# First stage of a two-layer backbone kernel: folds as rounded products, products streamed by tile, and the context's part moved

## The chip, the cores and the metric

One core of a Trainium2 chip runs the whole program. The metric is the device time of one execution in microseconds (us), and what is compared are medians over several executions. Beside them stands the trace of one profiled execution, whose span, from its first to its last instruction, is somewhat shorter than the device time.

## The reference, cut to what matters

The kernel computes two layers over 1024 latent tokens of 1024 channels, with 256 context tokens as a prefix. The change touches what comes first in the even layer: the modulation of both streams, the products of the input projection that it feeds, and the convolution and recurrence on them. It also touches one thing that belongs to the odd layer, the product of two weight matrices that are folded into one ahead of time (`w_in` with `w_grp`; pooling between them works along tokens only, so that they can be joined).

```python
sc, scc = silu(c), silu(c_ctx)
shift, scale, gate = split(sc @ mod_w[l] + mod_b[l], 3)
hx = rmsnorm(x, norm_g[l]) * (1 + scale) + shift
shift_c, scale_c, _ = split(scc @ mod_w[l] + mod_b[l], 3)
hc = rmsnorm(ctx, norm_g[l]) * (1 + scale_c) + shift_c
# even layer
va, vg, ga, xb, gb = split(hx @ w_in, 5)
y_a = silu(layernorm(conv31(va * sigmoid(vg)))) * silu(ga)
y_b = rglru(xb, h0=rglru_state(hc @ w_in_xb)) * silu(gb)
x = x + gate * (concat([y_a, y_b]) @ w_out)
# odd layer
u = hx1 @ w_in_u
y = (pool(u) - u) @ w_grp * scale * silu(g)
```

`rglru` is a short convolution of four taps, two gates from products with small matrices per head, and a scan in both directions; the latent scan starts from the state at which the context's ends.

## The kernel before

Channels lie on partitions: a tile is 128 channels by 1024 tokens, and KT = 8 of them make a stream. Exact enough products are made of rounded numbers (fp32r): both operands are split into a high part (a cast on ACT) and a low part (a subtraction on DVE or POOL), and three matmuls hi·hi, hi·lo and lo·hi are summed in PSUM. I call such a product a rounded triple. Some products are plain fp32 matmuls instead.

**The first stage** has an order that Tile's scheduler made from the code. It loads x tile by tile and sums its squares; broadcasts the silu of the two conditions c (cL for the latent, cC for the context) over the partitions with eight fp32r matmuls of one row; takes 24 dot products of a row block of `mod_w` with cL or cC on DVE (`modulation`, L353; twelve blocks, two conditions each) and computes the last two of each eight rows of shift and scale on PE (`mod_row`, L372 and L378); makes rstd of x as root products ms_x (L211); scales and shifts x into hi and lo parts h0h, h0l (`modulate`, L388 to L392); does the same for the context (`modulate_ctx`, L401 and L443); computes the decay rates of the recurrence (`decay_rates`, from L172); and folds two of four groups of the odd layer's weights in plain fp32 (`fold_whole`, L285; `grp` is graw, the other factor wu), which PE does whenever nothing else is ready. Then come the latent and context products of xb for j = 0 (L133 to L135).

**The loop over j = 0..7** has an order written by hand: `on(engine, ...)` issues each instruction behind the last one of its engine, and the profile puts all of it down to line L510, the line of that helper. A turn j runs on PE vg_j, va_j, xbc_{j+1} (the context's 256 columns), and then the gates of j between the products of xb_{j+1}. On DVE it does the four-tap convolution into uc, u_j = va · sigmoid(vg), the scans of tile j-1 and, in between, steps of the 31-tap convolution of earlier tiles. These steps are handed out by `fill(n)`: it runs n steps of whichever tile's convolution is under way, and does nothing as long as no tile is whole. The eight dots of the modulation's gate rows, on tiles called l, stand in turn j = 0.

Behind the loop come gb and wob products on PE with fixed `fill` counts in them. Where the layernorm of the convolution needs its mean, every step that is left is run:

```python
while ended[0] < KT:
    fill(1)
```

and `ln_mean` sums the eight tiles with a matmul called mu. From there on PE has nothing to do before that sum.

PSUM has eight banks: four in a rotating pool, a pair called xb (`wide`), and two single banks c0, c1, in which the convolution is summed. SP issues almost all DMA transfers; in the first stage `load` chains them in the order of the code.

Of the kernel before, what the change touches and what calls it, by code (L numbers as in the profile page):

```python
# [55 lines left out]
def body(ctx, tc, xT, ctxT, cc, ccol, modT, modW, win, gw, wout, wu, grp, wg, wo1, small, edge, ident, outT):  # L56
# [37 lines left out]

    def banks(name, n):
# [73 lines left out]
    def decay_rates():  # L169
        nc.scalar.activation(sa, lam, AF.Abs)  # L170
        nc.scalar.activation(sa, sa, AF.Exp, scale=-1.0)
        nc.vector.tensor_scalar(out=sb, in0=sa, scalar1=2.0, scalar2=None, op0=add)  # L172
        nc.vector.reciprocal(sb, sb)
        nc.vector.tensor_tensor(out=sz, in0=sa, in1=sb, op=mult)
        nc.vector.tensor_tensor(out=sb, in0=sz, in1=sz, op=mult)
        nc.vector.memset(sa, 1.0 / 17.0)
        for n in range(7, -1, -1):
            nc.vector.tensor_tensor(out=sa, in0=sa, in1=sb, op=mult)
            nc.vector.tensor_scalar(out=sa, in0=sa, scalar1=1.0 / (2 * n + 1), scalar2=None, op0=add)
        nc.vector.tensor_tensor(out=sa, in0=sa, in1=sz, op=mult)  # L180
        nc.vector.tensor_scalar(out=sb, in0=lam, scalar1=-1.0, scalar2=0.0, op0=mult, op1=ALU.max)
        nc.vector.scalar_tensor_tensor(out=sa, in0=sa, scalar=2.0, in1=sb, op0=mult, op1=add)
        nc.vector.tensor_scalar(out=chalf, in0=sa, scalar1=4.0, scalar2=None, op0=mult)
        nc.vector.tensor_scalar(out=cneg, in0=sa, scalar1=-8.0, scalar2=None, op0=mult)
# [86 lines left out]
    def fold_whole(g, out_tile, g_tile, w_tile):  # L271
        gs = []
        for i in range(2):
            raw = g_tile(f"graw_{g}_{i}")
            load(raw, grp[g, i])
            gs += [raw[:, 0:H], raw[:, H:D]]
        yield
        for kp in range(KT // 2):
            w = w_tile(f"wu_{g}_{kp}")
            load(w, wu[g, kp])  # L280
            for s in range(2):
                ps = psum(f"fold_{g}_{kp}_{s}")
                for i in range(4):
                    kc = slice(i * 2 * P + s * P, i * 2 * P + (s + 1) * P)
                    nc.tensor.matmul(ps, w[:, kc], gs[i], start=(i == 0), stop=(i == 3))  # L285
# [12 lines left out]
    cth = [cpool.tile([P, D], F32R, name=f"cth{i}") for i in range(2)]
    ctl = [cpool.tile([P, D], F32R, name=f"ctl{i}") for i in range(2)]
    cL = cpool.tile([P, D], F32, name="cL")  # L300
    hh, hl, ch, cl = [], [], [], []
    with ExitStack() as sctx:
        fpool = sctx.enter_context(tc.tile_pool(name="fpool", bufs=6))
        gpool = sctx.enter_context(tc.tile_pool(name="gpool", bufs=4))
        spool = sctx.enter_context(tc.tile_pool(name="spool", bufs=1))

        def fo_tile(name):
            return fpool.tile([P, H], F32, tag="fo", name=name)

# [24 lines left out]
        def sumsq(acc_, v, n, first, name, eng):
            if first:
                nc.scalar.activation(acc_[:, :n], v, AF.Square)
            else:
                q = ttile(name)
                nc.scalar.activation(q[:, :n], v, AF.Square)
                eng.tensor_tensor(out=acc_[:, :n], in0=acc_[:, :n], in1=q[:, :n], op=add)  # L340

        junk = spool.tile([P, D], F32, name="junk")

        def modulation(k, between=lambda: None):
            raws_ = []
            for m in (k, KT + k):
                raws_.append(dtile(f"mod0_{m}"))
                load(raws_[-1], modT[0, m])
                if m == k:
                    between()  # L350
            for m, raw in zip((k, KT + k), raws_):
                for i, vec in enumerate((cL, cC)):
                    nc.vector.scalar_tensor_tensor(out=junk, in0=raw, scalar=1.0, in1=vec, op0=mult, op1=mult,  # L353
                                                   accum_out=m0[:, i, m : m + 1])
            nc.vector.scalar_tensor_tensor(out=a0[:, :, k], in0=m0[:, :, KT + k], scalar=mb1[:, k : k + 1],
                                           in1=col(O_NG + k).to_broadcast([P, 2]), op0=add, op1=mult)
            v = m0[:, :, k]
            nc.vector.tensor_tensor(out=v, in0=v, in1=col(O_MB + k).to_broadcast([P, 2]), op=add)

        idx = spool.tile([P, P], F32, name="idx")
        ccv = spool.tile([P, KT, 2], F32, name="ccv")

        def mod_row(j):
            ps = psum(f"modr_{j}")[:2, : KR * P]
            for q in range(KT // KW):
                raw = dtile(f"modw_{j}_{q}")
                load(raw[:, : KW * KR * P], modW[j, q])
                for e in range(KW):  # L370
                    k = KW * q + e
                    nc.tensor.matmul(ps, ccv[:, k], raw[:, e * KR * P : (e + 1) * KR * P],  # L372
                                     start=(k == 0), stop=(k == KT - 1))
# [1599 lines left out]
```

## Time and profile before

| what | us |
|---|---|
| time, median of three executions (lowest to highest) | 1289.47 (1287.24 to 1290.38) |
| span of the profiled execution | 1287.8 |
| first fold matmul | starts at 8.97 |
| vg, va and xbc of j = 0 | 92.30, 105.96, 116.84 (start) |
| vg of j = 1 | 137.56 (start) |

A time is that of the device; the profile's own execution is one more run. Its page gives each engine's busy time, its share of the span and its number of instructions; the span in forty slices with a digit for tenths; and the chain of work that ended last, followed back from the end to whatever released each piece. A group names the source line, the engine, the operation, out<-in, the shape and the count, then total busy us, mean ns of one, and the idle time of that engine just before them with what ended it. In the time line of an engine a row is start, duration, what it is, and in square brackets the wait before it. A plain fp32 matmul of 512 columns leaves two records.

### The profile page before, as it was taken

What the parts mean: (1) busy time and instruction counts of PE and PEld (TensorE: products, weight loads), DVE (VectorE), ACT (ScalarE), POOL (GpSimd) and SP (SyncE); (2) the same over time, 40 slices, a digit from 0 to 9 for tenths busy, and PEclk for the clock granted to TensorE, in tenths of its full rate; (3) what the DMA queues carried; (4) which work ended last, traced back from release to release, by engine and by line L of the source; (5) the groups of instructions that cost most, each with busy time, mean ns of one, the idle gap of its engine ahead of it and who ended that gap; (6) DMA issues with size and microseconds to landing.
All of it is one profiled execution on the core that took longest, in us unless ns stands there. A gap on an engine that the chain in (4) does not pass through costs nothing.

```text
span 1287.8 us, 15841 instructions
## 1 busy us (share of the span) xinstructions
PE 1271.1 (99%) x5650; PEld 1027.5 (80%) x5650; DVE 1141.3 (89%) x1775; ACT 640.6 (50%) x941; POOL 354.3 (28%) x180
## 2 busy tenths in 40 slices
PE   8999999999999999999999999999999999999997
PEld 4468888888888888888887888888888888878886
DVE  7979999999999999988789667999999997887876
ACT  5343656666657623227426345834444444654543
POOL 3063655675558603443220023000000000000002
PEclk9999999999999999999999999999999999999999
DMA  9934111121212133543555356243333324777723
GB/s 371 358 114 157 58 41 63 44 74 42 66 41 90 50 115 107 168 147 113 172 174 192 127 185 203 87 155 127 110 132 131 123 96 157 245 247 258 296 83 131
DMA packets 83075, 181.87 MB, mean 141 GB/s; under 512 B 7858, under 2 KB 27826, under 8 KB 82996
## 3 DMA queue, kind: packets, MB, share of 16 engines
q1 hardware_dynamic: 74548, 176.67, 40.1%
q10 hardware_dynamic: 8448, 4.20, 1.1%
q8 instruction: 44, 0.72, 0.2%
q14 instruction: 35, 0.29, 0.1%
HBM read 136.79 MB, written 44.04 MB: 140 GB/s over the span
## 4 chain that ended last, share of the span: by engine, by line
PE 86%; DVE 6%; DMA 5%; ACT 1%; issue 1%; SPq 0%; POOL 0%; POOLq 0%; DVEq 0%; ACTq 0%
PE vg L510 7%; PE wob L510 7%; PE gb L510 7%; PE va L510 7%; PE xb L510 6%; PE g L510 4%; PE fold L285 3%; PE ga L510 2%; PE qb_v L1000 2%; PE qb_v L1001 2%; PE qb_v L998 2%; PE xbc L510 2%; PE qb_g L1000 2%; PE qb_g L1001 2%; PE qb_g L998 2%; DMA x<-xT 1%
## 5 line engine op out<-in xcount | busy, mean ns | idle before, releaser
L510 DVE SCALAR_TENSOR_TENSOR conv<-u,sm,conv 128x505 f32<-128x505 f32 (+6 forms) x224 | 153.9, 748 | 0.9
L1762 POOL TENSOR_TENSOR o<-x,rr 128x256 f32<-128x256 f32 (+1 forms) x10 | 9.4, 971 | 445.7 <-ACT rr L1698 443.8
L510 POOL TENSOR_TENSOR l<-l,l 128x1280 f32<-128x1280 f32 (+1 forms) x23 | 64.0, 2798 | 91.8 <-DVE l L510 65.5
L510 ACT ACTIVATE l<-g,sm 128x512 f32<-128x512 f32 (+1 forms) x96 | 58.7, 619 | 57.7 <-PE g L510 57.0
L285 PE MATMUL fold<-graw,wu 128*128 128x512 f32 x128 | 58.0, 614 | 2.3 <-DMA wu<-wu 2.3
L102 ACT CAST wq_g<-wr_g 128x512 fp32r<-128x512 f32 x48 | 28.3, 622 | 48.4 <-DVE wr_g L979 17.6
L285 PEld LDWEIGHTS fold<-graw,wu 128*128 128x128 f32 x128 | 25.1, 198 | 33.7 <-issue 32.7
L510 PE MATMUL vg<-h0h,wl_vg 128*128 128x512 f32 x128 | 50.0, 390 | 0.0
L510 PE MATMUL wob<-ybh,wh_wob 128*128 128x512 f32 x128 | 49.9, 390 | 0.0
L510 PE MATMUL vg<-h0h,wh_vg 128*128 128x512 f32 x128 | 49.8, 389 | 0.0
L510 PE MATMUL gb<-h0l,wh_gb 128*128 128x512 f32 x128 | 49.8, 389 | 0.0
L510 PE MATMUL gb<-h0h,wh_gb 128*128 128x512 f32 x128 | 49.8, 389 | 0.0
L510 PE MATMUL wob<-ybh,wl_wob 128*128 128x512 f32 x128 | 49.8, 389 | 0.0
L510 PE MATMUL vg<-h0l,wh_vg 128*128 128x512 f32 x128 | 49.8, 389 | 0.0
L510 PE MATMUL wob<-ybl,wh_wob 128*128 128x512 f32 x128 | 49.8, 389 | 0.0
L510 PE MATMUL va<-h0h,wh_va 128*128 128x512 f32 x128 | 49.8, 389 | 0.0
L510 PE MATMUL va<-h0l,wh_va 128*128 128x512 f32 x128 | 49.8, 389 | 0.0
L510 PE MATMUL va<-h0h,wl_va 128*128 128x512 f32 x128 | 49.8, 389 | 0.0
L510 PE MATMUL gb<-h0h,wl_gb 128*128 128x512 f32 x128 | 49.8, 389 | 0.0
L510 DVE TENSOR_TENSOR_SCAN l<-l,l 128x256 f32<-128x256 f32 (+1 forms) x32 | 48.7, 1521 | 1.1
L103 POOL TENSOR_TENSOR wl_wu<-wr_wu,wh_wu 128x1024 fp32r<-128x1024 f32 x8 | 19.2, 2417 | 106.9 <-ACT wh_wu L102 104.4
L510 POOL TENSOR_TENSOR l<-l,uc 128x1280 f32<-128x1280 f32 x16 | 48.1, 3032 | 0.0
(642 smaller groups left out, 4344.0 us busy)
## 6 DMA issues: line engine op xcount, KB each, us to landing
mod<-modT SPq DMA_DIRECT2D x20, 512.0 KB, 5.5
x_part<-xp SPq DMA_DIRECT2D x32, 256.0 KB, 3.1
mod<-modT SPq DMA_DIRECT2D x32, 256.0 KB, 3.1
wr_v<-wfold SPq DMA_DIRECT2D x16, 512.0 KB, 4.0
wr_g<-wg SPq DMA_DIRECT2D x16, 512.0 KB, 4.2
wr_wo<-wo SPq DMA_DIRECT2D x16, 512.0 KB, 4.6
y_b<-y SPq DMA_DIRECT2D x24, 256.0 KB, 3.4
y_t<-y SPq DMA_DIRECT2D x24, 256.0 KB, 2.9
```

What stands on the lines that cost most here:

```text
L102: return (nc.scalar.copy(hi, src), eng.tensor_tensor(out=lo, in0=src, in1=hi.bitcast(F32), op=sub))
L103: eng.tensor_tensor(out=lo, in0=src, in1=hi.bitcast(F32), op=sub))
L285: nc.tensor.matmul(ps, w[:, kc], gs[i], start=(i == 0), stop=(i == 3))
L510: last[eng] = f(*args, **kw)
L998: nc.tensor.matmul(ps, hi, xh[k], start=(first and k == 0), stop=False, skip_group_check=not first)
L1000: nc.tensor.matmul(ps, hi, xl[k], start=False, stop=False, skip_group_check=not first)
L1001: mm = nc.tensor.matmul(ps, lo, xh[k], start=False, stop=(k == KH - 1), skip_group_check=not first)
L1762: nc.gpsimd.tensor_tensor(out=outs[k // per][:, k % per], in0=x1[k][:, cols], in1=rr, op=mult)
```

## The change

1. The two folds become rounded triples: 192 fp32r matmuls where 64 fp32 ones were. `grp` and wu are split: casts on ACT, the four low parts of `grp` on DVE, the eight of wu on POOL.
2. c and c_ctx are broadcast by two DMAs of 512 KB, and their silu stays in PSUM (`cvec`), where the early dots read it; SBUF copies cL and cC serve the late ones. All modulation rows are dots on DVE, 32 of them; `mod_row` is gone.
3. xb0, vg0 and va0 run together as a stream over the eight x tiles, each tile's 18 matmuls as soon as its parts are there. For x tiles 1, 3 and 5 the high and low parts are made by two ACT operations and POOL.
4. The context's modulation, its xb products and its gates stand behind the latent gates of j = 0 and the products of xb1; vg1 is in front of these gates. The decay rates, wsum and the gate rows' dots come behind the stream.
5. The convolution's two banks are one tile `cw`. The loop starts at j = 1.
6. The whole of it goes through `on`, so that it has a written order on each engine. `fill` asks for 1 step in what was turn j = 0 (22 before) and for 20 in turn j = 1 (37 before). In the turns from j = 2 on, and behind the loop, it asks for what it asked before.

```diff
     def banks(name, n):
-        if n % 2:
-            t = wide(name)
-            return [t[:, h] for h in HALF]
-        return [pc.tile([P, H], F32, tag=f"c{i}", name=f"{name}_{i}") for i in range(2)]
+        t = wide(name) if n % 2 else wide2(name)
+        return [t[:, h] for h in HALF]
...
-                    nc.tensor.matmul(ps, w[:, kc], gs[i], start=(i == 0), stop=(i == 3))
...
+    def fold_part(n, s, part, between=()):
+        g = n // 4
+        w = fw[n][part == 2]
+        for i in range(4):
+            kc = slice(i * 2 * P + s * P, i * 2 * P + (s + 1) * P)
+            hi, lo = gpair[g][i // 2]
+            x = lo if part == 1 else hi
+            pe(fps_[n][s], w[:, kc], x[:, HALF[i % 2]], start=(part == 0 and i == 0), stop=(part == 2 and i == 3))
...
+    def split_w(name, out=None):
+        raw = wraw.pop(name)
+        hi, lo = out or [wpool.tile([P, D], F32R, tag=t, name=f"{t}_{name}") for t in ("wh", "wl")]
+        cast(hi, raw)
+        gp(out=lo, in0=raw, in1=hi.bitcast(F32), op=sub)
+        return hi, lo
...
+    def mod_dots(m, vecs=(0, 1)):
+        for i in vecs:
+            vec(nc.vector.scalar_tensor_tensor, out=mraw[m] if i else junk, in0=mraw[m], scalar=1.0,
+                in1=(cL, cC)[i] if late[0] else cvec[i], op0=mult, op1=mult, accum_out=m0[:, i, m : m + 1])
...
+    for k in range(KT):
+        if k < KT - 1:
+            scale_x(k + 1)
+            high_x(k + 1)
+        low_x(k)
...
+        for p, part in order:
+            (hi, lo), ps = prods[p]
+            for h in range(2):
+                pe(ps[h], (lo if part == 1 else hi)[:, kc], (hl if part == 2 else hh)[k][:, HALF[h]],
+                   start=(k == 0 and part == 0), stop=(k == KT - 1 and part == 2))
...
+    for m in (6, KT + 6, 7, KT + 7):
+        mod_dots(m, (1,))
+    mod_ready(1, 0, KT)
...
+    for h in range(2):
+        all_of(mm3_fixed(vg1[h], wnext_vg, (hh, hl), HALF[h]))
...
+    decay_rates()
...
+    at_rest()
+    fill(1)
+    xc = psum("xbc0")[:, :C]
+    all_of(mm3_fixed(xc, w, (ch, cl), slice(0, C)))
...
+    all_of(gate_steps(0, (gwh, gwl), (uh, ul), gates, ((0, C),)))
...
+    for j in range(1, KT):
...
-            fill(3)
+        fill(3 if j > 1 else 0)
...
-            fill(4)
+        fill(4 if j > 1 else 0)
...
-                fill((10, 6)[h])
+            fill((10, 6)[h] if j > 1 else 3)
...
-            fill(19 if state is None else 5 if final else 8)
+        fill(5 if final else 8)
```

The order of the instructions at three places follows. A row is line, operation, out<-in and shape; numbers behind names tell tiles apart, and `x2` stands for two in a row.

PE before, where the folds end and xb of j = 0 begins (all of h0h and h0l, for both halves, goes by before vg0):

```order
L285 MATMUL fold_3_1_644<-graw_0_425,wu_3_634 128x512 x2
L285 MATMUL fold_3_1_644<-graw_1_427,wu_3_634 128x512 x2
L133 MATMUL xb_680<-h0h_461,wh_xb_675 128x512
L134 MATMUL xb_680<-h0l_462,wh_xb_675 128x512
L135 MATMUL xb_680<-h0h_461,wl_xb_676 128x512
L133 MATMUL xb_680<-h0h_487,wh_xb_675 128x512
```

PE now, at the same place (ms_x is the root product of rstd, dg_x its diagonal from DVE; h0h_659 and h0h_679 are the high parts of x tiles 0 and 1):

```order
L274 MATMUL ms_x_589<-dg_x_621,ones 128x512
L274 MATMUL ms_x_590<-dg_x_624,ones 128x512
L274 MATMUL fold_1_588<-g1h_159,wl_571 128x512 x2
L274 MATMUL fold_1_588<-g1h_161,wl_571 128x512 x2
L274 MATMUL xb_685<-h0h_659,wh_xb_633 128x512 x2
L274 MATMUL vg_0_687<-h0h_659,wh_vg_643 128x512
L274 MATMUL vg_1_688<-h0h_659,wh_vg_643 128x512
L274 MATMUL va_686<-h0h_659,wh_va_661 128x512 x2
...
L274 MATMUL va_686<-h0h_659,wl_va_662 128x512 x2
L274 MATMUL xb_685<-h0h_679,wh_xb_633 128x512 x2
```

The root products have moved to the last quarter of the last fold, and behind it each product takes tile after tile instead of product after product.

DVE now, between two tiles of the stream (m_132 holds the modulation's rows, a_133 the scales, mod_5, mod_13 and mod_4 are row blocks):

```order
L274 SCALAR_TENSOR_TENSOR h0l_682<-x_202,m_132,h0h_659 128x1024
L274 SCALAR_TENSOR_TENSOR junk,m_132<-mod_5_580,cL 128x1024
L274 SCALAR_TENSOR_TENSOR x_359<-x_359,a_133,ms_x_589 128x512
L274 SCALAR_TENSOR_TENSOR x_359<-x_359,a_133,ms_x_590 128x512
L274 SCALAR_TENSOR_TENSOR junk,m_132<-mod_13_582,cL 128x1024
L274 SCALAR_TENSOR_TENSOR mod_4_519,m_132<-mod_4_519,cC 128x1024
```

The late dots, on cL and cC, have moved in between the parts that PE's stream takes.

DVE before, in turn j = 1, from u_0 on (u_861; uc_941 is the four-tap convolution of tile 1, the conv rows are the steps that `fill` hands out):

```order
L510 TENSOR_TENSOR u_861<-va_1_888,sg_1_801 128x512
L510 SCALAR_TENSOR_TENSOR edge_junk,edges<-u_861,sm 128x8
L510 TENSOR_TENSOR cL<-u_861 128x512
L510 TENSOR_SCALAR conv_0_943<-u_861,sm 128x512
L510 TENSOR_SCALAR conv_1_944<-u_861,sm 128x512
L510 SCALAR_TENSOR_TENSOR conv_0_943<-u_861,sm,conv_0_943 128x505
L510 SCALAR_TENSOR_TENSOR uc_941<-xbc_916,sm,uc_941 128x254
L510 SCALAR_TENSOR_TENSOR uc_941<-xbc_916,sm,uc_941 128x255 x2
L510 SCALAR_TENSOR_TENSOR conv_1_944<-u_861,sm,conv_1_944 128x504
```

DVE now, from u_0 (u_942) on:

```order
L274 TENSOR_TENSOR u_942<-va_686,sg_1_931 128x512
L274 SCALAR_TENSOR_TENSOR mod_6_647,m_132<-mod_6_647,cC 128x1024
L274 SCALAR_TENSOR_TENSOR mod_14_649,m_132<-mod_14_649,cC 128x1024
...
L274 SCALAR_TENSOR_TENSOR l_934,m_132<-l_934,cL 128x1024
...
L274 TENSOR_SCALAR sb<-sa 128x16
...
L274 TENSOR_TENSOR cL<-u_942 128x512
L274 TENSOR_SCALAR conv_1186<-u_942,sm 128x512
L274 SCALAR_TENSOR_TENSOR uc_928<-xbc_1188,sm,uc_928 128x254
```

Ahead of the first step of a convolution stand the context's dots, those with l and the decay rates; then one step, and the context's taps (uc_928<-xbc). Over the whole program both orders have 416 rows of convolution on DVE. From u_7 up to the layernorm's mean it is 197 rows before and 240 now, and the additions to lnsum there are 6 and 8.

More of the change, by code (lines that the diff above doesn't have):

```diff
@@ new lines, in square_add @@
+    def square_add(k, h):
+        f = dict(out=acc[h], in0=acc[h], in1=xq.pop((k, h)), op=add)
+        if h and k > 1 or k > 5:
+            vec(nc.vector.tensor_tensor, **f)
+        else:
+            gp(**f)
+    chain[0] = nc.sync.dma_start((graw.setdefault((0, 0), dtile("graw_0_0"))), grp[0, 0])
+    act(sb[:, 0:1], eps_l, AF.Silu)
+    busy = psum("busy")
+    for _ in range(20):
+        pe(busy[:, :P], ones, ones, start=True, stop=True)
+    load_g(0, 1)
+    load_fold(0)
+    load(cx[0], cc[0].partition_broadcast(P))
@@ new lines, in body @@
+    load_w("vg0", win[KT])
+    load_w("va0", win[0])
+    fold_out(5, 1)
+    fold_mm(6)
+    square(6)
+    square_add(6, 0)
+    square_add(6, 1)
+    square(7)
+    square_add(7, 0)
+    square_add(7, 1)
+    fw[7] = split_w(7)
+    fold_out(6, 0)
+    for t in range(4):
+        fold_store(t)
+    load_mod(5)
+    load_mod(KT + 5)
+    fold_out(6, 1)
+    mod_dots(4, (0,))
+    fold_banks(7)
+    rx = [psum(f"ms_x{h}") for h in range(2)]
+    n = H // P
+    fold_mm(7, range(5), {1 + h: [lambda h=h, c=c: pe(rx[h][:, c : c + 1], acc[h][:, c * P : (c + 1) * P],
+                                                      ones[:, 0:1], start=True, stop=True) for c in range(n)]
+                          for h in range(2)})
@@ new lines, in body @@
+    for h in range(2):
+        act(roots[:, h * n : (h + 1) * n], rx[h][:, :n], AF.Sqrt, bias=eps_r)
+    diags = []
+    for h in range(2):
+        r, t = roots[:, h * n : (h + 1) * n], ttile(f"dg_x{h}")
+        vec(nc.vector.reciprocal, out=r, in_=r)
+        vec(nc.vector.tensor_tensor, out=t.rearrange("p (c t) -> p c t", t=P),
+            in0=idx.unsqueeze(1).to_broadcast([P, n, P]), in1=r.unsqueeze(2).to_broadcast([P, n, P]), op=mult)
+        diags.append(t)
+    for h in range(2):
+        pe(rx[h], ones, diags[h], start=True, stop=True)
@@ new lines, in body @@
+    for i in range(2):
+        gp(out=ctl[i], in0=cx[i], in1=cth[i].bitcast(F32), op=sub)
+    load_w("va1", win[1], wr_tile("wr_va1"))
+    wva = split_w("va1", [xtile(f"w{i}_va1", F32R) for i in "hl"])
+    for m in range(2 * KT, 2 * KT + 4):
+        lrow_dots(m)
+        lrows[m + 4] = lrow(m + 4)
+    decay_rates()
+    vec(nc.vector.tensor_tensor, out=wsum, in0=taps[:, :, 0 : 2 * NT : 2], in1=taps[:, :, 1 : 2 * NT : 2], op=add)
+    L = [ltile(i, f"l{i}") for i in range(6)]
+    gates, roots = L[:4], L[4:]
@@ new lines, in body @@
+    xb = wide("xb1")
+    steps = (x for h in range(2) for x in mm3_fixed(xb[:, HALF[h]], wnext, (hh, hl), HALF[h]))
+    done = 0
+    for n, _ in enumerate(gate_steps(0, (gwh, gwl), (uh, ul), gates, ((C, H), (C + H, H)))):
+        while done < 16 * (n + 1) // 8:
+            next(steps)
+            done += 1
+    all_of(steps)
+    for m in range(2 * KT + 4, 3 * KT):
+        lrow_dots(m)
+    vec(nc.vector.tensor_tensor, out=m0[:, 0, 2 * KT :], in0=m0[:, 0, 2 * KT :], in1=col(O_MB + 2 * KT, KT), op=add)
@@ new lines, in body @@
+        (r0, i0, r1, i1), (e, f) = state[2], state[3]
+        gates, roots = [e, f, r0, r1], [i1, i0]
+        now = j, uc, gates, roots
+        done = 0
+        for n, _ in enumerate(gate_steps(j, (gwh, gwl), (uh, ul), gates)):
+            while done < 16 * (n + 1) // 12:
+                next(steps)
+                done += 1
+            if n == 9:
+                w = raw_split(raw, name)
+                rec_input(now, 0)
+        all_of(steps)
+        fill(5 if final else 8)
+        state, uc = now, ucn
```

893 lines of the change are left out of this document (485 added, 408 removed).

## The prediction

> **What bounds the kernel now.** I read the page first (busy time, the slices, the chain that ended last), then the chain piece by piece, the groups of instructions of the first 300 us, and at last the time lines of single engines where a term of the sum needs them.
>
> ```profile
> PE 1271.1 (99%) x5650; PEld 1027.5 (80%) x5650; DVE 1141.3 (89%) x1775; ACT 640.6 (50%) x941; POOL 354.3 (28%) x180
> ...
> PE   8999999999999999999999999999999999999997
> ...
> DVE  7979999999999999988789667999999997887876
> ...
> PE 86%; DVE 6%; DMA 5%; ACT 1%; issue 1%; SPq 0%; POOL 0%; POOLq 0%; DVEq 0%; ACTq 0%
> ```
>
> PE is busy 99% of the span, so time is won only by less work on PE and lost by every wait put on it. But DVE's digits are 9 in slices 4 to 16 as well (32.2 us each): from 130 to 547 us a second engine has no room either. That decides this case.
>
> PE's first stage, from the page, the chain, the groups and PE's time line:
>
> ```profile
> L285 PE MATMUL fold<-graw,wu 128*128 128x512 f32 x128 | 58.0, 614 | 2.3 <-DMA wu<-wu 2.3
> ...
> 46.27 27.66 PE fold L285 x64
> ...
> 148.44 10.88 PE va L510 x48
> ...
> 180.04 11.15 PE vg L510 x48
> ...
> L372 PE MATMUL modr<-modw,ccv 128*2 128x256 f32 x32 | 7.2, 379 | 0.0
> L378 PE MATMUL modt<-idx,modrow 2*128 2x2 f32 x8 | 1.2, 251 | 0.5 <-ACT modrow L375 0.5
> L211 PE MATMUL ms_x<-dg_x,ones 128*128 128x512 f32 x4 | 2.0, 618 | 1.5 <-DVE dg_x L208 1.5
> ```
>
> The va at 148.44 is that of j = 1, the vg at 180.04 that of j = 2. From va1 on both programs give PE the same matmuls in the same order, and from j = 2 on the loop is the same code. So the sum has two parts: when vg2 starts, and what is late after it.
>
> **What PE saves.** An fp32 fold matmul leaves two records: 128 at 27.66/64 = 0.432 us are 55.3 us. A rounded one costs 10.88/48 = 0.227 us; 192 are 43.5. Gain 11.8. The modulation rows go: 7.2 + 1.2 = 8.4. The waits for wu (2.3) and for modrow (0.5) go with their instructions. Together 23.0 us. The eight matmuls of the c broadcast ran before the first fold, which waited for its load; its operands are now split first, so I leave the fold's start alone (a us either way). With no new wait va1 would start at 148.4 - 23.0 = 125.4.
>
> **What it puts on DVE and POOL.** Eight more modulation dots (32 for 24), low parts of g on DVE, and of wu, xb0, vg0, va0 and three x tiles on POOL, beside each other. What that does, the trace shows at one place, in DVE's and POOL's time lines:
>
> ```profile
> 104.93 1.22 DVE L510 SCALAR_TENSOR_TENSOR l<-l,cL 128x1024 f32<-128x1024 f32 x1
> 106.07 3.98 DVE L510 SCALAR_TENSOR_TENSOR l<-l,cL 128x1024 f32<-128x1024 f32 x1
> 109.98 3.40 DVE L510 SCALAR_TENSOR_TENSOR l<-l,cL 128x1024 f32<-128x1024 f32 x1
> 113.31 2.30 DVE L510 SCALAR_TENSOR_TENSOR l<-l,cL 128x1024 f32<-128x1024 f32 x1
> ...
> 105.31 3.66 POOL L510 TENSOR_TENSOR ul<-uc,uh 128x1280 fp32r<-128x1280 f32 x1 [3.32 <-ACT uh L510]
> 108.92 3.38 POOL L510 TENSOR_TENSOR wl_xb<-wr_xb,wh_xb 128x1024 fp32r<-128x1024 f32 x1
> 112.26 2.27 POOL L510 TENSOR_TENSOR wl_gw<-wr_gw,wh_gw 128x512 fp32r<-128x512 f32 x1
> ...
> 124.58 14.76 DVE L510 SCALAR_TENSOR_TENSOR conv<-u,sm,conv 128x504 f32<-128x504 f32 x22
> ...
> 134.99 2.41 POOL L510 TENSOR_TENSOR wl_vg<-wr_vg,wh_vg 128x1024 fp32r<-128x1024 f32 x1 [20.45 <-ACT wh_vg L510]
> ```
>
> Alone a dot takes 1.22. Beside POOL the same dot takes 2.3 to 4.0, and each POOL subtraction is about one dot longer than alone (2.37, below): they run in turn. The convolution taps, whose sum is in PSUM, keep 14.76/22 = 0.67, and POOL's 2.41 at 134.99 is as short beside them as anywhere. So I count **in turn** what DVE does from SBUF alone and all of POOL, and leave out DVE operations with an operand in PSUM. By the taps' row the early dots, which read c from PSUM, are free; the late ones, on cL and cC, are not. [...]
>
> Prices of the pieces, from the groups by shape:
>
> ```profile
> L388 DVE SCALAR_TENSOR_TENSOR x<-x,a,ms_x 128x512 f32<-128x512 f32 x16 | 10.8, 744 | 0.5 <-PE ms_x L211 0.5
> L392 DVE SCALAR_TENSOR_TENSOR h0l<-x,m,h0h 128x1024 fp32r<-128x1024 f32 x8 | 10.5, 1335 | 0.0
> L443 DVE TENSOR_TENSOR cx<-cx,ssqc 128x1024 f32<-128x1024 f32 x2 | 2.4, 1222 | 0.0
> L178 DVE TENSOR_TENSOR sa<-sa,sb 128x16 f32<-128x16 f32 x8 | 1.4, 175 | 0.3
> L103 POOL TENSOR_TENSOR wl_xb<-wr_xb,wh_xb 128x1024 fp32r<-128x1024 f32 x1 | 2.4, 2371 | 0.0
> L401 POOL TENSOR_SCALAR cx<-cx,a,m 128x256 f32<-128x256 f32 x8 | 5.2, 670 | 7.6 <-DVE cx L443 7.6
> L340 POOL TENSOR_TENSOR ssq<-ssq,xsq 128x512 f32<-128x512 f32 x7 | 10.3, 1473 | 18.2 <-ACT xsq L339 18.1
> L391 ACT ACTIVATE h0h<-x,m 128x1024 fp32r<-128x1024 f32 x8 | 9.1, 1147 | 6.5 <-DVE x L388 6.3 <-DMA wfold<-fo 0.2
> L510 ACT ACTIVATE l<-l,cneg 128x1280 f32<-128x1280 f32 x8 | 10.5, 1361 | 0.0
> L510 ACT ACT_TABLE_LOAD x13 | 16.7, 1283 | 0.2
> L510 POOL TENSOR_TENSOR l<-l,l 128x1280 f32<-128x1280 f32 x8 | 23.6, 2965 | 11.6 <-ACT l L510 11.6
> ```
>
> **New waits of PE, one by one**, each as its two ends and the value taken.
>
> Folds: PE waits where a weight's low part is later than the 5.4 us (24 x 0.227) of matmuls on the weight before. POOL needs 2.4 for one and has the square sums of x besides, up to 1.5 each, in turn with DVE's splits and sums. It keeps up on average, not at each weight. 0 to 4; I take 2.
>
> Start of the stream: the root products of rstd are now queued ahead of the last quarter of the last fold. Behind them DVE scales two halves (2 x 0.74) and ACT makes the first high part (1.15): 2.6, with the fold's 0.9 as cover, and the second vg bank waits for the cast of the last fold, behind that on ACT (about 1). 2 to 3.5; 2.5.
>
> Stream: 144 matmuls are 32.6 us. In turn beside them stand on POOL seven low parts (16.6) and the four sums of the context's squares (three of 1.5 at most, one of half that: 4.5), on DVE five low parts and ten late dots (15 x 1.22 = 18.3; their 1.34 in the groups holds waiting) and some small ones (1): 40.4. The scaling of x (14 x 0.74 = 10.4) reads ms_x in PSUM and runs beside POOL. Each tile needs its two dots, its scaling and its parts in that order, so PE waits for the sum: 40.4 - 32.6 = 8. Without taking turns DVE's 30 and POOL's 21 both fit under PE's 32.6. 0 to 9; 8.
>
> Context: xbc0 and the context gates of j = 0 found their input ready; the work on it lay under the folds and xb0. Now it stands behind the stream, and in DVE's fixed order so do the dots with l and decay_rates, all ahead of the context's taps. Counted in turn: on DVE four ctx dots and eight with l (12 x 1.22 = 14.6), two scalings (2.4), some 30 of 0.175 (5); on POOL the low parts of xb1 and va1 (4.7), of u and the gate weights (3.0 and 1.2, by width), the eight adds (5.4) and two low parts of the context (4.8): 41 us, of which a little lies after the gates. PE has 33.0 of work there (vg1 10.9, gates and xb1 16.3, xbc 5.7). That is 6 to 8. Dots, adds, casts, xbc, taps, cast of u, low part and gates follow each other through four engines, which adds some microseconds, while the evictions of the latent gates are queued on ACT behind the two context casts, so that PE's banks come free late. With the order of before, 0; by this count up to 16; I take 11.
>
> Gates of j = 1: queued behind them on PE is all of j = 2. They wait for the recurrence of j = 0, which must give its buffers back: two tanh, two exp, two roots (6 x 1.36), two table loads (2.6), two squares on POOL (5.9): 16.7 us from the context gates on. Before, vg1 and va1 (21.8) lay over that; now vg1 has been moved ahead and only va1 and an xbc (13.8) are left. 0 to 4; 3.5.
>
> DMA: the stage loads the same sixteen modulation tiles' worth (twelve and four of modW before), and two broadcasts of c more, 512 KB each. They are hidden as long as about 37 transfers of 0.52 MB arrive before the stream, near 60 us; at the rate of the next row they take 47.5. Were that cover gone, va0 would be late by the difference, a few us. I take 0. SP's stores of the last folds stand ahead of the loads of vg1 and xb1, which have 20 us to spare.
>
> ```profile
> 30.00:40.00 10.00, 8.46 (x40) 4.31 (x39) 9.65 (x23) 2.65 (x5) 0.00 (x0) 1.00 1.03 408
> ```
>
> (A row of the table by stretch: busy us of PE, its loads, DVE, ACT and POOL, the granted clock, the DMA share, GB/s.)
>
> Sum 2 + 2.5 + 8 + 11 + 3.5 = 27.0; 27.0 - 23.0 = **+4**: vg2 at 184.
>
> **What is late after vg2.** The convolution is done on DVE in steps that `fill` hands out; up to the end of j = 1 there were 59, now 21. No later fill is larger. The 38 steps, and two additions to the layernorm sums that were POOL's, come where everything is emptied: ahead of the layernorm mean. DVE's and PE's time lines there:
>
> ```profile
> 414.66 0.69 DVE L510 TENSOR_TENSOR u<-va,sg 128x512 f32<-128x512 f32 x1 [0.81 <-PE va L510]
> ...
> 531.96 18.95 DVE L510 SCALAR_TENSOR_TENSOR conv<-u,sm,conv 128x505 f32<-128x505 f32 x28
> ...
> 565.54 3.13 DVE L510 TENSOR_TENSOR lnsum<-lnsum,u 128x512 f32<-128x512 f32 x2
> ...
> 569.11 0.69 DVE L510 TENSOR_TENSOR mu0l<-lnsum,mu0h 128x512 fp32r<-128x512 f32 x1
> ...
> 573.67 0.39 PE L510 MATMUL mu<-mu0h,ones_r 128*128 128x512 f32 x1
> ```
>
> At 414.66 DVE waits for va7: it is level with PE there, so what it was spared in j = 0 and 1 is no lead that it could still have. A step is 18.95/28 = 0.677; 38 are 25.7, the two additions 1.4: 27.1. DVE had the mean ready at 569.8, PE came for it at 573.7: 3.9 are free. So 23.2; the lnsum pair took 3.13 instead of 1.4 beside POOL, which would then be idle: 21.4. I take 22, from 18.5 (DVE also uses its short waits there) to 23.5. All of PE's wob is issued by then, so it stands.
>
> [...]
>
> **Sum.** The profiled span is 1287.8, 1.7 under the median of 1289.5. 1287.8 + 4 + 22 + 1.7 = **1316** (rounded up from 1315.5).
>
> **Rivals.** A: DVE and POOL hardly hinder each other in the new order. Stream 0, context 2: 2 + 2.5 + 2 + 3.5 - 23 = -13, vg2 at 167; the mean still waits: 1289.5 - 13 + 22 = **1298**. For it: taps and scaling are exempt, the first dots read PSUM. Against: the rows at 106 to 116.
> B, faster: the written order keeps PE fed. The stage's saving stands (23, and 1 from an earlier first fold), the gates of j = 1 are covered, and the mean waits 18.5: 1289.5 - 24 + 18.5 = **1284**. It decides where va1 starts: in this case at 124.4; each us later is one lost, and past 126 nothing measurable is left. For it: PE waited little in the stage of before. Against: 16.7 us of gate chain over 13.8 of PE, which ask for 3 alone.
> C: as B, but with the mean's wait at its full 23.5 us: 1289.5 - 24 + 23.5, about **1290**, no change.
> D: the stage doesn't do what the title says; the order starves PE at every step, all terms at their upper ends: 36.5 - 23 = 13.5 and 23.5 at the mean: **1327**.
>
> **Chances.** Forecast (1306 to 1325) 0.62, A (1292 to 1305) 0.19, C 0.07, B 0.07, D 0.05. The range 1292 to 1325 leaves out B, C and D, a little under 0.2. A measurement tells 0.3% (3.9 us) from no change: faster 0.07, same 0.07, slower 0.86.
>
> **What would show it.** Folds of 192 records at 0.23; va1 near 149 (A: 132, B: 124); dots of 2 to 4 us on cL and cC between 60 and 130; an idle PE ahead of the context gates; one wait of about 22 us ahead of `mu`, released by DVE. Were that wait missing, the step on the deferred convolution would be wrong, whatever the total.

## The result, and the profile after

| | time, us (lowest to highest) | span of the profiled execution |
|---|---|---|
| before | 1288.43 (1287.24 to 1290.38) | 1287.8 |
| changed | 1353.38 (1351.39 to 1359.61) | 1352.2 |

The change makes the kernel slower: the ratio is 1.051, with an interval of 1.0484 to 1.0535. The median of before is here that of four executions, one more than in the table ahead of the prediction. The direction was forecast, the size was not: 1353 lies beyond the 1327 of the worst rival.

The page of the changed kernel, the lines that answer to those shown of before, and the granted clock:

```profile
PE 1270.8 (94%) x5700; PEld 1046.8 (77%) x5700; DVE 1189.1 (88%) x1793; ACT 652.2 (48%) x947; POOL 378.8 (28%) x186
...
PE   8987989989999999972999999999999999999997
...
DVE  5898799999999999999868975998999998787976
...
PEclk9989999999999999995999999999999999999999
...
PE 58%; DVE 19%; issue 9%; ACT 5%; POOL 4%; DMA 4%; SPq 0%; POOLq 0%; ACTq 0%; DVEq 0%
```

PE is busy for as long as before in a span that is 64.4 us longer, and its share of the chain falls from 86% to 58%; DVE's rises from 6% to 19%. The digits 7 and 2 in PE's row are a hole near 600 us. The view of the waits names the holes (PE's line, who released it, us in total, times, longest):

```profile
PE mu L274 <- DVE mu0h L274: 34.8, 1, 34.8
PE vg L274 <- POOL wl_vg L274: 9.7, 5, 3.5
PE g L274 <- ACT l L274: 9.2, 2, 7.9
PE xb L274 <- POOL h0l L274: 4.8, 1, 4.8
PE gb L274 <- POOL wl_gb L274: 3.2, 1, 3.2
```

Two of these stand in no term of the prediction: weights' low parts late for vg, five times, and for gb. Cut at PE's landmarks (starts from PE's time line, us), the 64.4 us lie here:

| stretch | before | after | more | forecast |
|---|---|---|---|---|
| start to vg of j = 2 | 179.9 | 186.1 | 6.2 | 4 |
| turns j = 2 to 7, to the start of gb | 234.9 | 251.2 | 16.3 | 0 |
| gb and wob, to the wait ahead of `mu` | 158.9 | 162.5 | 3.6 | 0 |
| the wait ahead of `mu` | 0.0 | 34.8 | 34.8 | 22 |
| from `mu` to the end | 714.1 | 717.6 | 3.5 | 0 |

The rows at which the turns begin and end, of before and then of after:

```profile
179.88 0.39 PE L510 MATMUL vg<-h0h,wh_vg 128*128 128x512 f32 x1
...
414.74 0.40 PE L510 MATMUL gb<-h0h,wh_gb 128*128 128x512 f32 x1
```

```profile
186.12 0.39 PE L274 MATMUL vg<-h0h,wh_vg 128*128 128x512 f32 x1
...
437.31 0.40 PE L274 MATMUL gb<-h0h,wh_gb 128*128 128x512 f32 x1
```

The row of the turns starts the search. From j = 2 on both programs give PE the same matmuls and ask for the same `fill`. Yet this is how DVE ran the steps of the long convolution there, in time lines of one turn (start, duration, and the count that the row gathers):

```profile
229.25 10.04 DVE L510 SCALAR_TENSOR_TENSOR conv<-u,sm,conv 128x504 f32<-128x504 f32 x15
```

That was before; this is after:

```profile
242.75 11.79 DVE L274 SCALAR_TENSOR_TENSOR conv<-u,sm,conv 128x511 f32<-128x511 f32 x15
```

10.04/15 = 0.669 a step, and now 11.79/15 = 0.786. The groups give one step a mean of 750 ns either way: no step became longer, but they no longer overlap. DVE's written order tells why, here three rows of tile 3 of before and three of after (the number behind a name tells buffers apart; DVE counts on a semaphore what it has done, and in square brackets stand the count that the row waits for and the one to which it raises it):

```
SCALAR_TENSOR_TENSOR conv3_0_2235<-u3_1867,sm_115,conv3_0_2235 128x505 [waits for 345, raises to 347]
SCALAR_TENSOR_TENSOR conv3_1_2236<-u3_1867,sm_115,conv3_1_2236 128x504 [waits for 346, raises to 348]
SCALAR_TENSOR_TENSOR conv3_0_2235<-u3_1867,sm_115,conv3_0_2235 128x506 [waits for 347, raises to 349]

SCALAR_TENSOR_TENSOR conv3_2674<-u3_1966,sm_115,conv3_2674 128x505 [waits for 368, raises to 369]
SCALAR_TENSOR_TENSOR conv3_2674<-u3_1966,sm_115,conv3_2674 128x504 [waits for 369, raises to 370]
SCALAR_TENSOR_TENSOR conv3_2674<-u3_1966,sm_115,conv3_2674 128x506 [waits for 370, raises to 371]
```

The rows go by turns to the left and the right half of the sum. Before, these halves were two tiles, and a step waited for the step two rows back: the row that raises the count to 347 waits for 345. As one tile `cw` each step waits for the row just ahead of it, though the halves share no element. My theory after the result: 0.12 us a step is lost there, which a DVE that is busy 155 of 160 us has no room for; POOL's low parts, queued behind additions that wait for DVE's scans, get late, and PE waits. The rival was that the deferred steps and the first stage alone make the time.

One such wait, in the time line of POOL and then of PE:

```profile
276.22 2.37 POOL L274 TENSOR_TENSOR l<-l,l 128x1024 f32<-128x1024 f32 x1 [16.44 <-DVE l L274]
278.56 2.35 POOL L274 TENSOR_TENSOR wl_vg<-wr_vg,wh_vg 128x1024 fp32r<-128x1024 f32 x1
```

```profile
277.11 0.39 PE L274 MATMUL vg<-h0l,wh_vg 128*128 128x512 f32 x1
280.96 0.50 PE L274 MATMUL vg<-h0h,wl_vg 128*128 128x512 f32 x1 [3.46 <-POOL wl_vg L274]
```

POOL stands idle for 16.44 us with the low part of vg's weight next in its queue, until DVE's scan lets the addition ahead of it go; the low part ends at 280.9 and PE's third matmul goes.

### The profile page after: what moved, and what is told of

The parts are those of the page before. It is cut to its first block, busy times and chain, and to the rows that moved or that the text cites. A ratio compares the mean times of both kernels' runs of the same rounds, so it can differ in the third digit from the quotient of the medians.

```text
span 1352.2 us, 15957 instructions
## 1 busy us (share of the span) xinstructions
PE 1270.8 (94%) x5700; PEld 1046.8 (77%) x5700; DVE 1189.1 (88%) x1793; ACT 652.2 (48%) x947; POOL 378.8 (28%) x186
## 4 chain that ended last, share of the span: by engine, by line
PE 58%; DVE 19%; issue 9%; ACT 5%; POOL 4%; DMA 4%; SPq 0%; POOLq 0%; ACTq 0%; DVEq 0%
DVE conv L274 6%; PE vg L274 5%; POOL l L274 2%; PE wob L274 2%; ACT l L274 2%; PE va L274 2%; PE ga L274 2%; PE ga L131 2%; PE ga L129 2%; PE ga L130 2%; PE qb_g L1204 1%; PE qb_g L1206 1%; PE qb_g L1207 1%; PE qb_v L1204 1%; PE qb_v L1207 1%
## 5 line engine op out<-in xcount | busy, mean ns | idle before, releaser
L274 DVE SCALAR_TENSOR_TENSOR conv<-u,sm,conv 128x505 f32<-128x505 f32 (+6 forms) x224 | 168.0, 750 | 6.4
L274 PE MATMUL xb<-h0l,wh_xb 128*128 128x512 f32 x128 | 50.3, 404 | 5.3 <-POOL h0l L274 4.8
L274 DVE SCALAR_TENSOR_TENSOR conv<-cL,wsum,conv 128x506 f32<-128x506 f32 (+3 forms) x70 | 52.5, 750 | 2.2
L274 PE MATMUL xb<-h0h,wh_xb 128*128 128x512 f32 x128 | 49.9, 400 | 1.9 <-ACT h0h L274 1.9
L274 PE MATMUL xb<-h0h,wl_xb 128*128 128x512 f32 x128 | 49.7, 398 | 0.0
```

What stands on the lines that cost most here:

```text
L274: last[eng] = f(*args, **kw)
```

## The experiments

### The first four: the tile, the deferred steps, and the turn-taking

**e1_two_banks** is the changed kernel with the convolution's sum in two one-bank tiles again. Only the stream's product at the start still uses the wide tile, from a pool that is closed before the first convolution.

```diff
     def banks(name, n):
-        t = wide(name) if n % 2 else wide2(name)
-        return [t[:, h] for h in HALF]
+        if n % 2:
+            t = wide(name)
+            return [t[:, h] for h in HALF]
+        return [pcs[0].tile([P, H], F32, tag=f"c{i}", name=f"{name}_{i}") for i in range(2)]
...
+    pwide.close()
+    pcs[0] = ctx.enter_context(tc.tile_pool(name="pcs", bufs=1, space=PSUM))
```

> The changed kernel with one thing undone: the convolution is summed in two separate single-bank tiles again instead of in the two halves of one tile cw. Theory S (serial steps: with one tile each step of the convolution waits for the step just before it, 0.78 us apart instead of 0.67): steps come 0.67 apart again, vg2 stays near 186, the turns j = 2 to 7 shrink from 44 to 47 us to about 43, PE's wait ahead of mu falls from 34.8 to about 20, and the time from 1353 to 1318 to 1328. Theory F (the late start of the turns and POOL's late weight parts make the loop slow, whatever the steps take): turns stay at 44 to 47, the time stays at 1345 to 1355.

Measured: 1332.09 us (1331.31 to 1332.46), ratio 1.032 (1.0297 to 1.0343). So 21.3 us of the loss come from the tile. Thirteen steps ahead of `mu`, in DVE's time lines, first of the changed kernel and then of this one:

```profile
620.94 10.19 DVE L274 SCALAR_TENSOR_TENSOR conv<-u,wsum,conv 128x505 f32<-128x505 f32 x13
```

```profile
599.09 8.59 DVE L279 SCALAR_TENSOR_TENSOR conv<-u,wsum,conv 128x505 f32<-128x505 f32 x13
```

The step is back at 8.59/13 = 0.66.

The table by stretch has for 240 to 400 us first the changed kernel, then this one (busy us and count of PE, its loads, DVE, ACT and POOL, the granted clock, the DMA share, GB/s):

```profile
240.00:400.00 160.00, 153.00 (x723) 126.76 (x722) 155.12 (x197) 93.64 (x105) 96.76 (x41) 0.99 0.16 53
```

```profile
240.00:400.00 160.00, 160.00 (x774) 135.19 (x773) 155.12 (x207) 98.31 (x113) 97.81 (x41) 1.00 0.16 53
```

DVE is busy for the same 155.12 us in both, with 197 rows done in one and 207 in the other. A busy share can't show this loss; the count beside it can. The view of the waits has for `mu` and vg:

```profile
PE mu L279 <- DVE mu0h L279: 27.4, 1, 27.4
PE vg L279 <- POOL wl_vg L279: 2.7, 1, 2.7
```

The waits at vg fell from 9.7 in five to 2.7 in one. The wait ahead of `mu` fell from 34.8 to 27.4, not to the 20 or so that I had from the prediction.

**e2_before_one_tile** does that one part alone, in the kernel before.

```diff
-        return [pc.tile([P, H], F32, tag=f"c{i}", name=f"{name}_{i}") for i in range(2)]
+        t = pc.tile([P, S], F32, tag="cw", name=name)
+        return [t[:, h] for h in HALF]
```

> The kernel before with one part of the change alone: the convolution's two banks as the halves of one tile. Theory S: 416 steps at 0.11 us more are 45 us of DVE, of which its idle time up to the layernorm (about 11) and the slack of 3.9 take some; steps 0.78 apart, a wait ahead of mu of 10 to 25 us, the time 1310 to 1325. Theory F: the bank's shape costs nothing, 1286 to 1292.

Measured: 1321.56 us (1319.14 to 1322.17), ratio 1.0235 (1.0215 to 1.0256): 32 us for an edit that changes no number and, but for two small matmuls that swap places near 3.5 us, no order. The place of the sum doesn't change either: every tile is summed in PSUM's banks 4 and 5 in both kernels, so the steps differ only in what they wait for. Its view of the waits:

```profile
PE vg L511 <- POOL wl_vg L511: 9.9, 4, 3.0
PE mu L511 <- DVE mu0h L511: 6.0, 1, 6.0
```

The waits at vg are those of the changed kernel (9.7). vg of j = 2 starts at 179.8 as before, and gb 20.2 us later than before. That the tile costs 32 us here and 21 in the changed kernel stands in the turns, by PE's landmarks: from vg of j = 2 to gb it adds 20.3 us here and 12.0 there. Why was not followed up.

**e3_before_fewer_fills** takes the term of 22 us alone: the kernel before, with `fill` asked for as the change asks (1 in turn 0, 20 in turn 1).

```diff
-            fill(3)
+            fill(3 if j > 1 else 0)
...
-            fill(4)
+            fill(4 if j > 1 else 0)
...
-                fill((10, 6)[h])
+                fill((10, 6)[h] if j > 1 else 3)
...
-            fill(3)
+            fill(3 if j else 0)
...
-            fill(19 if state is None else 5 if final else 8)
+            fill(1 if state is None else 5 if final else 8)
```

> The kernel before with another part alone: fill asks for 1 step in turn j = 0 and 20 in turn j = 1, as in the changed kernel, and 38 steps are left for the end. As predicted: vg2 stays at 180, one wait of 18.5 to 23.5 us ahead of mu, the time 1308 to 1314. If DVE makes the steps up on the way: under 1300.

Measured: 1320.08 us (1315.13 to 1322.31), ratio 1.0222 (1.0193 to 1.0252). PE's time line has the wait, 23.94:

```profile
596.62 0.80 PE L510 MATMUL mu<-mu0h,ones_r 128*128 128x512 f32 x1 [23.94 <-DVE mu0h L510]
599.14 0.63 PE L510 MATMUL wob<-ybh,wh_wob 128*128 128x512 f32 x1
...
602.54 0.40 PE L510 MATMUL wob<-ybh,wl_wob 128*128 128x512 f32 x1
```

The wait is right to 2 us; the time is 6 above what I expected of it. Some of that stands in the same rows: the matmuls behind the wait take 0.63 to 0.80 where 0.39 is usual, and the next landmark, the first `ga`, comes 28.1 us behind `mu` instead of 25.5. This kernel scatters over 7 us, and its profiled span, 1313.3, is that of its fastest execution.

**e4_lows_on_dve** is the changed kernel with the low parts of x tiles 1, 3 and 5 on DVE and their high parts by one ACT operation, as for the even tiles.

```diff
-        if k % 2 and k < 7:
+        if False:
             act(xs[k], xs[k], AF.Identity, bias=m0[:, 0, k : k + 1])
...
-        if k % 2 and k < 7:
+        if False:
             gp(out=hl[k], in0=xs[k], in1=hh[k].bitcast(F32), op=sub)
```

> The changed kernel with the high part of x tiles 1, 3 and 5 by one ACT operation and their low part on DVE like the others, not on POOL. If DVE (from SBUF) and POOL run in turn: three POOL operations of 2.4 us leave, three DVE ones of 1.2 come, the wait of 4.8 us for h0l goes and the stream (43.7 us from 62.3 to 106.0) ends 3 to 6 us earlier; va1 at 147 to 150. If they do not hinder each other: DVE has 3.6 us more on its own path, the stream ends 1 to 4 us later. In both the time moves less than that, since DVE sets the end of the turns: 1346 to 1356.

Measured: 1347.96 us (1346.48 to 1350.76), ratio 1.0446 (1.0423 to 1.047). va of j = 1 starts at 147.7 instead of 152.8, and PE's waits for the low parts of x fall from 4.83 in one piece to 3.9 in four. The work given to POOL to relieve DVE came with a loss of 5 us. This edit also takes one ACT operation off each of the three tiles, so that the price of POOL alone is not shown; but PE's waits for ACT's high parts are 1.9 us in both kernels, and it is the wait for POOL that goes.

### The next four: what can be won back, and two readings tested

**e5_fills_back** is e1 with turn j = 1 asking again for what it asked before.

```diff
-        fill(3 if j > 1 else 0)
+        fill(3)
...
-        fill(4 if j > 1 else 0)
+        fill(4)
...
-            fill((10, 6)[h] if j > 1 else 3)
+            fill((10, 6)[h])
```

> The changed kernel with two separate banks for the convolution, and fill in turn j = 1 as in the kernel before (37 steps instead of 20). The 17 steps are 11.5 us of DVE. If DVE has spare time before vg2 (it waits for ACT 8 us between 148 and 171): vg2 stays within 3 us of 185.5, the wait ahead of mu falls from 27.4 to about 16, the time from 1332 to 1319 to 1324. If DVE is full there: vg2 comes 8 to 12 us later, the wait ahead of mu still falls, and the time stays at 1328 to 1335.

Measured: 1318.37 us (1315.63 to 1320.15), ratio 1.0222 (1.0202 to 1.0242). The wait ahead of `mu` falls from 27.4 to 11.1, by 16.3:

```profile
PE mu L279 <- DVE mu0h L279: 11.1, 1, 11.1
```

Against this, vg of j = 2 comes 7.0 later (192.5 for 185.5): 17 steps are back in a turn where DVE is not free either. This lies between the two cases expected: vg of j = 2 moved by more than 3 us, and yet the time fell. Of the 16.3, the 17 steps are some 11.3 (at 0.66); the additions to the layernorm sums just ahead of the mean make most of the rest, four that take 2.6 us where e1 has six that take 7.4. Net, 13.7 of the 42 us that e1 was slower than before come back.

**e6_repaired** adds e4's edit, and moves the low parts of the odd half's products (`ybl`, ahead of the last stretch) from DVE to POOL.

```diff
-        if k % 2 and k < 7:
+        if False:
...
-            vec(nc.vector.tensor_tensor, out=tl[:, HALF[h]], in0=y, in1=th[:, HALF[h]].bitcast(F32), op=sub)
+            gp(out=tl[:, HALF[h]], in0=y, in1=th[:, HALF[h]].bitcast(F32), op=sub)
```

> The kernel of the run before with two more repairs: the low parts of x tiles 1, 3 and 5 on DVE, and the sixteen low parts of the gated recurrence (ybl, 0.6 us each on DVE) on POOL. If the parts add up: 5 us less from the first (as measured alone), 10 us less DVE work ahead of the layernorm's mean from the second, so 12 to 15 us under the run before, 1305 to 1312. If the steps put back have only moved the wait into the first stage, DVE's relief still counts: 1313 to 1320.

Measured: 1313.29 us (1311.43 to 1313.75), ratio 1.0186 (1.0171 to 1.0201). This is the best version of the change that I found: 40 us faster than the changed kernel, and still 1.9% slower than before. The 5 us against e5 are e4's; the wait ahead of `mu` stayed at 11.1, so the relief of DVE by `ybl` bought nothing.

**e8_lows_on_pool** asks that by itself: e3 with `ybl` on POOL. I had read the wait ahead of `mu` as the sum of DVE's work.

> The kernel before with fewer fills, and the sixteen low parts ybl on POOL instead of DVE. If the wait ahead of mu is the sum of DVE's work (my reading): 9.8 us less on DVE, the wait falls from 23.9 to 13 to 16 and the time by 8 to 11 us. If it is the position of the deferred steps that counts, whatever else DVE does: the wait stays over 20.

Measured: 1315.41 us (1314.13 to 1318.93), ratio 1.0209 (1.0191 to 1.0227), and a wait of 23.94, to the hundredth that of e3. My reading fell. DVE's time line shows what it did with the time:

```profile
506.00 0.69 DVE L510 TENSOR_TENSOR yr<-yr,sb 128x512 f32<-128x512 f32 x1 [5.28 <-DMA yr<-yb_raw]
...
516.54 0.69 DVE L510 TENSOR_TENSOR yr<-yr,sb 128x512 f32<-128x512 f32 x1 [6.63 <-DMA yr<-yb_raw]
...
518.00 1.80 DVE L510 TENSOR_TENSOR yr<-yr,sb 128x512 f32<-128x512 f32 x1
```

It waits for `yr` to come back from memory, and its last `yr` starts at 518.0; in e3, with 16 subtractions more, at 517.9. What is spared ahead of that point is lost in these waits. So what counts for the mean is what stands behind the last `yr`: 63 steps before, 101 in e3, e1 and the changed kernel, 84 in e5 (counted in DVE's time lines up to the first cast of the mean, `mu0h`). The 38 steps that the change defers, and the 17 that e5 puts back, stand there in full.

**e7_kept_busy** and **e9_busy_to_the_end** measure what a wait costs behind its end. e3 gets matmuls ahead of `mu` whose result nothing reads, 90 in e7 and, since those ended too early, 118 in e9.

```diff
             ln_sums()
+            idle = psum("idle")
+            for _ in range(90):
+                on("pe", nc.tensor.matmul, idle, ones_r, hh[0][:, HALF[0]], start=True, stop=True)
```

> The kernel before with fewer fills, and 90 matmuls more ahead of mu whose result nobody reads, so that PE works through most of its wait (20.4 of 23.9 us). If a long wait halves PE's clock for some microseconds after it: mu's matmuls start 0.23 apart instead of 0.4 to 0.8, the first ga comes 25.6 us behind mu instead of 28.1, the granted clock there is 1.0 instead of 0.94, and the time is 2 to 5 us under the run with fewer fills alone. If the clock has nothing to do with the wait: the same time within 2 us, the same distance to ga.

> As the run that kept PE busy ahead of mu, with 118 idle matmuls instead of 90 (26.8 us), so that they end when the mean is ready, not 7 us before. If a pause halves the clock: mu's matmuls and the first wob behind them start 0.23 apart, the first ga comes 25.6 us behind mu (28.1 and 28.5 in the two runs before), the granted clock behind mu is 1.0. If the halved clock there has another cause: 28 us again.

e7: 1316.52 us (1316.09 to 1317.81), ratio 1.0215 (1.02 to 1.023). The idle products ended near 594, a wait of 6.81 was left, and the first `ga` came 28.5 us behind `mu`: the short wait cost as much behind it as the long one. For the question it was inconclusive. e9: 1316.32 us (1315.93 to 1317.66), ratio 1.0199 (1.0171 to 1.0226), without a wait. The stretch around `mu`, of e3 and then of e9 (the columns of the table by stretch, above):

```profile
596.00:604.00 8.00, 7.38 (x19) 5.22 (x20) 7.79 (x15) 3.69 (x6) 0.00 (x0) 0.59 0.01 2
```

```profile
596.00:604.00 8.00, 8.00 (x36) 6.57 (x35) 6.13 (x11) 2.19 (x4) 0.00 (x0) 1.00 0.01 2
```

PE's granted clock is 0.59 behind the wait and 1.00 without it, with nearly twice the matmuls in the same 8 us, and `ga` follows `mu` by 24.9 us instead of 28.1. So this wait costs 3.2 us beyond its own length. The total shows no gain that the intervals tell apart, since the 118 products themselves end late: `mu` starts at 600.4 instead of 596.6.

### The last one: the context's casts

PE waits 7.93 us in the gates of j = 0. ACT's time line of the changed kernel shows the two context casts, which wait for DVE, ahead of the evictions that free PE's banks:

```profile
129.07 1.04 ACT L274 CAST cth<-cx 128x1024 fp32r<-128x1024 f32 x1 [11.41 <-DVE sa L274]
131.21 1.04 ACT L274 CAST cth<-cx 128x1024 fp32r<-128x1024 f32 x1 [1.10 <-DVE sa L274]
...
133.11 3.11 ACT L274 ACTIVATE l<-g,sm 128x512 f32<-128x512 f32 x5
```

**e10_casts_behind** is e1 with these casts behind the gates. (Its POOL subtractions move with them.)

```diff
-        cast(cth[i], cx[i])
-    for i in range(2):
-        gp(out=ctl[i], in0=cx[i], in1=cth[i].bitcast(F32), op=sub)
     load_w("va1", win[1], wr_tile("wr_va1"))
...
     all_of(steps)
+    for i in range(2):
+        cast(cth[i], cx[i])
+    for i in range(2):
+        gp(out=ctl[i], in0=cx[i], in1=cth[i].bitcast(F32), op=sub)
```

> The changed kernel with two separate banks, and with the two casts of the context and its low parts issued behind the latent gates of j = 0 instead of ahead of them; nothing else moves. PE's wait of 7.9 us for ACT in these gates goes either way. If it was only ACT's queue: va1 starts 6 to 9 us earlier than 152.2 and the time falls by as much as vg2 does, to 1322 to 1328. If the context's chain through DVE and POOL is what ends last: the wait comes back ahead of xbc or the context gates, va1 starts within 3 us of 152.2, and the time stays at 1328 to 1335.

Measured: 1330.68 us (1328.78 to 1332.4), ratio 1.0307 (1.0282 to 1.0332), no difference from e1 that the intervals tell apart. The wait of 7.93 is gone, and PE's time line has others in its place:

```profile
135.32 0.39 PE L279 MATMUL xbc<-cth,wh_xb 128*128 128x256 f32 x1 [0.35 <-ACT cth L279]
...
137.74 0.58 PE L279 MATMUL xbc<-ctl,wh_xb 128*128 128x256 f32 x1 [2.04 <-POOL ctl L279]
...
148.65 0.58 PE L279 MATMUL g<-uh,wh_gw 128*128 128x256 f32 x1 [3.63 <-ACT uh L279]
```

va of j = 1 starts at 152.0, with the casts ahead at 152.2. Behind the wait that was named stood the next links of the same chain: `ctl` comes behind POOL's additions for the context, and ACT's cast `uh` itself waits 5.45 us for DVE's taps, which stand behind the dots with l. The context's chain decides, not ACT's queue.

## Why the prediction was right or wrong, step by step

**The savings of PE and the first stage: near, a little short.** vg of j = 2 came 6.2 us later than before, forecast 4. From PE's time line: the folds waited 3.3 (forecast 2); the start of the stream 2.4 (2.5); the stream took 43.7 for 32.6 of matmuls and so lost about 11 (8), with one long wait of 4.83 for POOL's h0l; the context's stretch took 46.9 for 34.4 and lost 12.5 (11; its 33.0 of work left out the 1.4 of the context gates); the gates of j = 1 lost 1.7 (3.5). The folds started 0.9 earlier. Rival A wanted va of j = 1 at 132 and B at 124; it came at 152.8, forecast 149. The dots beside POOL are as forecast, DVE's and POOL's time lines:

```profile
63.88 3.41 DVE L274 SCALAR_TENSOR_TENSOR junk<-mod,cL 128x1024 f32<-128x1024 f32 x1
```

```profile
63.26 2.95 POOL L274 TENSOR_TENSOR wl_va<-wr_va,wh_va 128x1024 fp32r<-128x1024 f32 x1 [0.38 <-ACT wh_va L274]
66.15 3.40 POOL L274 TENSOR_TENSOR h0l<-x,h0h 128x1024 fp32r<-128x1024 f32 x1
```

The dot, 1.22 alone, takes 3.41 and ends at 67.3, 1.1 us behind the end of the first POOL operation at 66.2; the second one, 2.40 alone (the h0l at 75.80), takes 3.40 and ends at 69.6, 2.3 us behind the dot. These ends are those of a run in turn. e4's 5 us agree with a price on the turns, though its edit spares ACT three operations as well.

**The clock behind a wait: left out, and it was a term.** The prediction's sum has nothing for it. PE's time line behind the wait in the context's stretch:

```profile
133.84 0.80 PE L274 MATMUL g<-uh,wh_gw 128*128 128x512 f32 x1 [7.93 <-ACT l L274]
134.44 0.63 PE L274 MATMUL g<-ul,wh_gw 128*128 128x512 f32 x1
...
139.13 0.48 PE L274 MATMUL xb<-h0h,wh_xb 128*128 128x512 f32 x1
139.45 0.39 PE L274 MATMUL xb<-h0l,wh_xb 128*128 128x512 f32 x1
```

For 5.3 us, at a granted clock of 0.50, matmuls go 0.43 apart instead of 0.227. Thirteen are issued where 23 could be: 2.3 us. In the stream the same spacing is seen behind the 2.4 us at its start (granted clock 0.56 from 64.05 to 67.90) and behind h0l's wait (0.50 from 93.63 to 97.30), which together cost some 3.7 us, and behind `mu` e3 and e9 put it at 3.2 us. So the first stage holds about 6 us of low clock, and yet it overshot by only 2.2: by this count, without the clock the stream and the context would have lost about 7 and 10 us, less than the 8 and 11 taken, and the gates of j = 1 lost less as well. That vg of j = 2 came near the forecast is in part luck.

**"From j = 2 on the loop is the same code": the step that failed.** It held for the matmuls and for `fill`'s numbers, not for `banks`, a helper that the change touches far from the loop. The edit was listed in the change and given no price. Shown by e1 (21.3 us back) and e2 (32 us from it alone). It took the 0.677 us that a step takes on two tiles for a step on one, and no row that the prediction shows is of a joined tile. In the changed kernel it is most of the turns' 16.3 (waits at vg 9.7, 3.3 of lower clock behind two of them; without the tile 4.3 are left in all), the 3.6 at gb and wob (0.2 left), and 7.4 of the wait ahead of `mu`.

**The deferred convolution: right mechanism, 22 forecast, 23.9 alone.** e3 shows the wait, released by DVE at `mu`, half a us over the upper end of 18.5 to 23.5. In the changed kernel it is 34.8: 7.4 by the tile, as e1 shows, and 3.5 between e1 and e3. Those rows differ in the additions to the layernorm sums, two pairs of which take 2.71 and 3.41 in e1, beside POOL's additions to xp and low parts of the wob weights, and 1.29 and 1.28 in e3. That is read from the rows and was not tried. The basis holds: all 38 steps stand behind the last `yr` (101 for 63), where DVE's own work sets the mean, and the stretch from there to `mu0h` grew from 49.5 to 78.2 us. What the prediction did not say is that only work behind that point may be summed so: e8 shows that DVE gives up in waits whatever it is spared ahead of it.

**The sum.** 1316 was forecast; without the tile it is e1's 1332, which is still above the range's 1325. The 16 us between, by e1's profile: 1.5 at vg of j = 2, 4.3 in the turn behind it, where one wait of 2.74 and the clock hold vg up, 0.2 at gb and wob, 5.4 in the wait ahead of `mu` and 4.9 behind it. The tile's 21 make the rest. e5 and e6 say where it could be won back: about 14 by the fills, 5 by the low parts. No version beat the kernel before. e6's remaining 24 us lie at the same places (6.2 at vg of j = 2, 2.6 and 0.2 behind it, 11.1 ahead of `mu`, 4.2 behind it), and whether another order of the context's chain would win them is open. Of the 4 to 5 us behind `mu`, about 2 stand ahead of the first `ga` (27.7 us behind `mu` in e1 and 27.4 in e6, 25.5 before), where e9 shows the clock; the rest wasn't followed.

## What to carry to other kernels

In these kernels a tile is the unit of dependency: joining two buffers into one, without touching a single instruction, tied alternate steps into one chain (0.79 us a step for 0.67; 21.3 us in e1, 32 in e2), so price a change of a helper at every place that calls it and not only in the stage that is rewritten. On an engine that is 97% busy compare counts of finished instructions over the same stretch, since here the busy time was the same 155.12 us while the work fell behind, 197 rows for 207. And deferred work cost what of it landed behind the last point at which its engine waited for something else (38 steps, and a wait of 23.94 in e3 as in e8, which has 16 subtractions fewer on DVE ahead of that point); find that point before summing durations.

## What the runs showed of the hardware that was not expected

On about 512 columns with the sum in PSUM, DVE took 0.79 us for a step that waits for the step just before it (11.79 us for 15, changed kernel) and 0.67 for one that waits for the one two back (10.04 for 15, before), while one record lasts 0.75 in both.

The granted clock fell also behind a short wait, and not behind a longer one. In e1 a wait of 2.74 us at vg of j = 2 was followed by seven matmuls 0.43 apart, at a granted clock of 0.57 in this row of the table by stretch:

```profile
189.00:193.00 4.00, 4.00 (x11) 3.13 (x12) 4.00 (x6) 2.31 (x2) 4.00 (x2) 0.57 0.38 131
```

In the changed kernel a longer wait, the 3.46 us at 280.96, was followed by none, with matmuls 0.23 apart at a granted clock of 1.00:

```profile
281.00:285.00 4.00, 4.00 (x18) 3.29 (x19) 3.86 (x7) 2.31 (x2) 4.00 (x2) 1.00 0.37 131
```

No run here shows why the shorter wait was followed by a low clock and the longer one was not.
